# Convolution tail and conditioning units of a four-layer encoder trunk: second matrix fetched inside the channel blocks, partial sums multiplied as one chain

## The chip, the core and the metric

One core of a Trainium2 chip runs the whole program in one launch. The metric is the device time of that launch in microseconds (us), as the median of several runs. TensorE is written PE in the profile (PEld is its weight load), VectorE DVE, ScalarE ACT, GpSimd POOL and SyncE SP; SP issues nearly all of the DMAs.

## What is computed

The reference runs four layers over 256 tokens of 1024 channels. The mixer of a layer is attention (layers 0 and 3), a Conformer convolution module (layer 1) or a causal pooling mixer (layer 2); after each mixer comes a feed-forward block (FF) of 4096 channels with a squared ReLU. Each sub-layer adds `gate * rmsnorm(y)` to x and starts from `rmsnorm(x) * (1 + scale) + shift`; shift, scale and gate of all layers come from one conditioning vector:

```
c_act = silu(c)
mod = c_act @ ada_w[i] + ada_b[i]            # (1024) @ (1024, 6144), each layer
sh_m, sc_m, gt_m, sh_f, sc_f, gt_f = split(mod, 6)
# convolution module
a = h @ w_pw1 + b_pw1
u = a[:, :D] * sigmoid(a[:, D:])
u = causal_depthwise_conv(u, w_dw, width 31) + b_dw
u = silu(layernorm(u, ln_g, ln_b))
y = u @ w_pw2 + b_pw2
```

## The kernel before

**Products.** Every weight tile (128 x 1024, float32) is fetched into one of five `raw` buffers (`fetch`, L155) and split by `load` into a high part (ACT, L173) and a low part (DVE, L174); six buffers hold high parts, six low parts. A product is three matmuls: high times high, low times high, high times low (`mm3`, L583, L586 and L587).

**Conditioning units.** The matrix `ada_w` is read in units of 128 rows by 2048 columns (1 MB each, four `araw` buffers, L197). Eight units make a group, a group makes one row of shift, scale or gate values. `ada(n, vec)` takes n units. A unit outside `vec` is multiplied on PE at once (`ada_mm`, L265): four matmuls j = 0 to 3, each with a 32-column weight tile, into four partition strips of one bank of PSUM. A unit inside `vec` is added on DVE to two running sums `acc` (first half of the columns, then second half, L221 and L223), and `ada_flush` multiplies these sums by ones with the same four matmuls; j // 2 picks the half. `ada_fetch(n)` issues the DMAs of n units; `ada` issues one itself when none is waiting. A flush comes at the end of a group, and wherever a stretch that keeps sums on DVE ends. The tables `MIX` and `FF` say how many units each part takes: a list (for FF, one number for each of its 16 chunks; for the convolution, one for each of its eight channel blocks and one for its tail), then the units in the boundary ahead of the part, then the units fetched ahead near its end. In every boundary the units are multiplied on PE. 88 units are consumed in all.

**Feed-forward.** Each chunk c makes 256 hidden channels: two columns of h (L652 and L655, `colhalf`), relu and square on ACT, the split into `gh` and `gl`, the units of that chunk behind it on DVE, then the product with w2 of the chunk before (L583 to L587, `y`). At chunk 14 (`CF`) the units of the next part are fetched ahead. Boundary: the squares of y, the update of x, the norm, and the transposes into the next input (`transposed0`, L395; `transposed1`, L412).

**Convolution.** Eight channel blocks m. In each: fetch of the first matrix's tile of block m + 2; the product (`colblock`, L600 to L606); sigmoid (L1095) and gate (L1097); the block is written to DRAM and read back shifted as `u4` (L1100, L1079) one block later; the depthwise taps of an earlier block (L1060) and their transposes into token order, `ctok` (L1065); the units; and the broadcast of the gate row once it exists (`gate_row`). The tail has the taps of the last two blocks for each half t of the tokens, the LayerNorm (statistics L1126 and L1128, root on POOL L115 and L121, `un` L1132), transposes (L1149), Silu (L1155), the split (L1158, L1159) and the second matrix in two `rowblock`s of four tiles. The bias `b_pw2` is split like a weight and put into `y` by two matmuls with one row of ones for each quarter of y (L1143, L1144).

**Order of the work.** SP issues in the order of the text. On the other engines a planner orders the instructions at build time by its own cost figures and by their place in the text; `nosync(a, b)` and `line(engine, a)` put a behind b on its engine without a semaphore. An engine runs its instructions in the order so made.

Of the kernel before, what the change touches and what calls it, by code (L numbers as in the profile page):

```python
# [16 lines left out]
ALU = mybir.AluOpType  # L17
# [6 lines left out]
NT = S // P  # L24
KT = D // P
# [26 lines left out]
def tile_trunk(ctx: ExitStack, tc: tile.TileContext, x, cT, pos, invf, ada_w, ada_bg,  # L52
# [100 lines left out]
    def fetch(src):  # L153
        raw = raws.tile([P, D], F32, tag="raw", name="raw")[0:src.shape[0], 0:src.shape[1]]
        nc.sync.dma_start(raw, src)  # L155
        fetched[(src.tensor.name, src.offset)] = raw
# [3 lines left out]
    def load(src, pre=None, lined=False):  # L160
        key = (src.tensor.name, src.offset)
        if key in loaded:
            return loaded.pop(key)
        o = (slice(0, src.shape[0]), slice(0, src.shape[1]))
        if key not in fetched:
            fetch(src)
        raw = fetched.pop(key)
        if pre is not None:
            pre(raw)
        h = his.tile([P, D], F32R, tag="hi", name="hi")[o]  # L170
        l = los.tile([P, D], F32R, tag="lo", name="lo")[o]
        put = (lambda ins, eng: line(eng, ins)) if lined else after
        put(A.copy(h, raw), "act")  # L173
        put(V.tensor_tensor(l, raw, h.bitcast(F32), op=ALU.subtract), "dve")  # L174
        gate["free"] -= 1
        return h, l


    rows = {}
# [80 lines left out]
    def ada_mm(lhsT, raw, stop):  # L260
        first = "pt" not in grp
        if first:
            grp["pt"] = bank("ada", "adap")
        for j in range(4):
            mm = T.matmul(grp["pt"][32 * j:32 * j + 32, :], lhsT, raw[j // 2][:, HALF[j % 2]],  # L265
                          start=first, stop=stop)
            if gate["pe"] is not None:
                nosync(mm, gate["pe"])
        gate["ada"] = mm
# [66 lines left out]
    def prep(row):  # L336
        bcast("a", row, 1)
        bct["sh"] = row
# [701 lines left out]
    def conv(i, h, units, ahead, first):  # L1040
        j = i // 3
        hh, hl = h
        with tc.tile_pool(name=f"conv{i}", bufs=1) as vp:
# [42 lines left out]
            for m in range(KT):  # L1086
                if m + 2 < KT:
                    for p in range(2):
                        fetch(w_pw1[j, m + 2, p])
                if m == 0:  # L1090
                    hb = turned(first, vp.tile([P, 512], F32, tag="uc", name="r0", bufs=2), A.copy)
                else:
                    hb = colblock(w_pw1[j, m], hh, hl, "pw1")
                sg = vp.tile([P, S], F32, tag="sg", name="sg", bufs=2)
                sgi = A.activation(sg, hb[:, S:], AF.Sigmoid, bias=vecs["b1"][:, 8 + m:9 + m])  # L1095
                u = up[m % 3]
                V.scalar_tensor_tensor(u[:, 30:286], hb[:, :S], vecs["b1"][:, m:m + 1], sg,  # L1097
                                       op0=ALU.add, op1=ALU.mult)
                ud = dr.tile([4, 32, 288], F32, tag="ud", name="ud")
                nc.sync.dma_start(ud.rearrange("b r t -> (b r) t"), u)  # L1100
                uds.append((m, ud))
                if m > 0:
                    pend.append(spread_taps(*uds.pop(0)))
                if m > 0:
                    dgs.append(diags(m - 1))
                if len(pend) == 2:
                    taps(*pend.pop(0), dgs.pop(0), 0, S)
                ada(units[m], vec=ALL)
                gate_row(i)
            pend.append(spread_taps(*uds.pop(0)))  # L1110
            dgs.append(diags(KT - 1))
            b2h, b2l = load(b_pw2[j])
            wp = [load(w_pw2[j, k]) for k in range(4)]
            nosync(A.activation(vp.tile([P, 1], F32, name="warm"), vecs["lb"][:, 0:1], AF.Silu),
                   sgi)
            for t in range(NT):
                for p, dg in zip(pend, dgs):
                    taps(*p, dg, t * P, P)
            prep(rows[(i, 2)])
            shift_rows()  # L1120
            sh_, sl_ = planes()
            un = []
            for t in range(NT):
                st = sm.tile([P, 2, 6], F32, tag="st", name="st")
                for n in range(2):
                    V.bn_stats(st[:, n], ctok[t][n])  # L1126
                mv = sm.tile([P, 2], F32, tag="mv", name="mv")
                V.bn_aggr(mv, st)  # L1128
                r = rsqrt_eps(mv[:, 1:2])
                xn = tmp.tile([P, D], F32, tag="xa", name="un")  # L1130
                for n in range(2):
                    V.tensor_scalar(xn[:, 512 * n:512 * n + 512], ctok[t][n], mv[:, 0:1], r,  # L1132
                                    ALU.subtract, ALU.mult)
                un.append(xn)
            ada(units[8])
            ada_flush()
# [1 line left out]
            y = y_banks()  # L1138
            for t in range(NT):
                ts = slice(t * P, (t + 1) * P)  # L1140
                for n in range(2):
                    ns = slice(512 * n, 512 * n + 512)
                    T.matmul(y[t][n], ones_r, b2h[:, ns], start=True, stop=False, skip_group_check=True)  # L1143
                    T.matmul(y[t][n], ones_r, b2l[:, ns], start=False, stop=False, skip_group_check=True)  # L1144
                for g in range(2):
                    b = bank("h", "sT_ps")
                    for k in range(4):
                        kk = 4 * g + k
                        T.transpose(b[:, k * P:(k + 1) * P], un[t][:, kk * P:(kk + 1) * P], ident)  # L1149
                    sv = vp.tile([P, 4, 264], F32, tag="u4", name="sv", bufs=3)  # L1150
                    sv = sv.rearrange("p a b -> p (a b)")[:, 0:512].rearrange("p (a b) -> p a b",
                                                                              a=4)
                    for k in range(4):
                        kk = 4 * g + k
                        A.activation(sv[:, k], b[:, k * P:(k + 1) * P], AF.Silu,  # L1155
                                     scale=vecs["lg"][:, kk:kk + 1], bias=vecs["lb"][:, kk:kk + 1])
                    o = (slice(None), slice(4 * g, 4 * g + 4), ts)
                    V.tensor_copy(sh_[o], sv)  # L1158
                    V.tensor_tensor(sl_[o], sv, sh_[o].bitcast(F32), op=ALU.subtract)  # L1159
            rowblock(wp, [sh_[:, k] for k in range(4)],  # L1160
                     [sl_[:, k] for k in range(4)], y, False, False, tiles_first=True)
            ada_fetch(ahead)
            rowblock([w_pw2[j, 4 + k] for k in range(4)], [sh_[:, 4 + k] for k in range(4)],
                     [sl_[:, 4 + k] for k in range(4)], y, False, True)
# [12 lines left out]
    def pool(i, head, consts, units, ahead):  # L1177
# [87 lines left out]

    MIX = {
        0: ([2, 4, 2, 3, 3, 2], 0, 1),
        1: ([0, 0, 2, 0, 1, 2, 1, 0, 1], 2, 3),
        2: (2, 4, 3),
        3: ([0, 0, 0, 0, 0, 0], 0, 0),  # L1270
    }
    FF = {
# [3 lines left out]
        3: ([0] * NFC, 0, 0),  # L1276
    }
    qgs = cp.tile([P, q_g.shape[0], 3], F32, name="qgs")
# [139 lines left out]
```

## Time and profile before

| | |
|---|---|
| runs, us | 1173.12, 1180.72, 1184.35; median 1180.72 |
| profiled execution, us | 1184.47, span 1182.6 |
| PE busy | 1138.4 us, 96% of the span |
| PEld busy | 923.5 us, 78% |
| DVE busy | 850.6 us, 72% |
| ACT busy | 645.3 us, 55% |
| POOL busy | 54.1 us, 5% |
| mean granted TensorE clock | 0.983 |
| DMA | 290.00 MB, mean 245 GB/s |

The busy share says which engine is nearly always in use; where in the span it is not, and where it works at a lower clock, is seen only by stretches. The ends of matmuls in the profile are modelled, so the distance from one start to the next is the better measure of PE's pace.

### The profile page before, as it was taken

What the parts mean: (1) busy time and instruction counts of PE and PEld (TensorE: products, weight loads), DVE (VectorE), ACT (ScalarE), POOL (GpSimd) and SP (SyncE); (2) the same over time, 40 slices, a digit from 0 to 9 for tenths busy, and PEclk for the clock granted to TensorE, in tenths of its full rate; (3) what the DMA queues carried; (4) which work ended last, traced back from release to release, by engine and by line L of the source; (5) the groups of instructions that cost most, each with busy time, mean ns of one, the idle gap of its engine ahead of it and who ended that gap; (6) DMA issues with size and microseconds to landing.
All of it is one profiled execution on the core that took longest, in us unless ns stands there. A gap on an engine that the chain in (4) does not pass through costs nothing. (4 is left out here: it accounts for less than half of the span.)

```text
span 1182.6 us, 17593 instructions
## 1 busy us (share of the span) xinstructions
PE 1138.4 (96%) x6706; PEld 923.5 (78%) x6706; DVE 850.6 (72%) x1197; ACT 645.3 (55%) x1145; POOL 54.1 (5%) x127
## 2 busy tenths in 40 slices
PE   7899999999999999999999999999997999999997
PEld 4667778788778867888887677878877878888886
DVE  3689787877766665787876778787876995755554
ACT  3355576556553244755564366555545675756553
POOL 1000010000010010000000110000011001000000
PEclk9999999999999988999999899999998999999999
DMA  9878759787617785778896479888644522766550
GB/s 332 304 290 311 298 208 347 270 329 290 245 53 236 256 322 213 272 272 351 315 343 256 187 278 364 311 311 323 246 134 157 170 81 80 250 199 191 183 193 35
DMA packets 73383, 290.00 MB, mean 245 GB/s; under 512 B 9986, under 2 KB 15234, under 8 KB 61012
## 3 DMA queue, kind: packets, MB, share of 16 engines
q1 hardware_dynamic: 70484, 280.44, 65.1%
q0 software_dynamic: 2816, 8.46, 2.0%
q8 instruction: 52, 0.85, 0.3%
q14 instruction: 31, 0.25, 0.1%
HBM read 286.57 MB, written 2.29 MB: 244 GB/s over the span
## 5 line engine op out<-in xcount | busy, mean ns | idle before, releaser
L174 DVE TENSOR_TENSOR lo<-raw,hi 128x1024 fp32r<-128x1024 f32 (+2 forms) x335 | 392.0, 1192 | 98.4 <-ACT hi L173 69.0
L173 ACT CAST hi<-raw 128x1024 fp32r<-128x1024 f32 (+2 forms) x335 | 335.1, 1028 | 78.6 <-PE y L587 39.4
L652 PE MATMUL h<-hT,hi 128*128 128x512 f32 x960 | 240.4, 392 | 0.0
L652 PEld LDWEIGHTS h<-hT,hi 128*128 128x128 f32 x960 | 175.8, 188 | 37.7 <-issue 3.4
L583 PE MATMUL y<-hi,gh 128*128 128x512 f32 x512 | 200.3, 393 | 1.5 <-ACT hi L173 1.5
L586 PE MATMUL y<-lo,gh 128*128 128x512 f32 x512 | 200.1, 391 | 0.2
L587 PE MATMUL y<-hi,gl 128*128 128x512 f32 x512 | 199.0, 390 | 0.0
L655 PEld LDWEIGHTS h<-hT,lo 128*128 128x128 f32 x960 | 131.0, 190 | 14.9 <-issue 5.9
L704 ACT COPY r<-h 128x256 f32<-128x256 f32 x120 | 44.5, 371 | 175.8 <-PE h L655 175.7
L655 PE MATMUL h<-hT,lo 128*128 128x256 f32 x960 | 136.0, 283 | 0.0
L223 DVE SCALAR_TENSOR_TENSOR acc<-araw,c_act,acc 128x1024 f32<-128x1024 f32 x106 | 130.7, 1279 | 0.4 <-DMA araw<-in_ada_w_dram 0.4
L583 PEld LDWEIGHTS y<-hi,gh 128*128 128x128 f32 x512 | 96.3, 188 | 22.8 <-ACT hi L173 2.4
L587 PEld LDWEIGHTS y<-hi,gl 128*128 128x128 f32 x512 | 96.1, 188 | 21.8 <-issue 0.8
L586 PEld LDWEIGHTS y<-lo,gh 128*128 128x128 f32 x512 | 96.4, 188 | 18.5 <-DVE lo L174 1.0
L705 DVE TENSOR_TENSOR r<-h,r 128x256 f32<-128x256 f32 x120 | 50.5, 421 | 39.8 <-ACT r L704 39.2
L710 DVE TENSOR_TENSOR gl<-r,gh 128x512 fp32r<-128x512 f32 x60 | 41.4, 690 | 50.2 <-ACT gh L709 50.2
L706 ACT ACTIVATE r<-r 128x512 f32<-128x512 f32 x60 | 37.9, 632 | 35.2 <-DVE r L705 35.2
L583 PE MATMUL y<-hi,hT 128*128 128x512 f32 x96 | 39.4, 412 | 0.0
L707 ACT ACTIVATE r<-r 128x512 f32<-128x512 f32 x60 | 37.9, 632 | 1.7
L586 PE MATMUL y<-lo,hT 128*128 128x512 f32 x96 | 38.8, 405 | 0.0
L587 PE MATMUL y<-hi,hT 128*128 128x512 f32 x96 | 38.6, 404 | 0.0
L709 ACT CAST gh<-r 128x512 fp32r<-128x512 f32 x60 | 37.2, 620 | 1.4
(257 smaller groups left out, 1486.8 us busy)
## 6 DMA issues: line engine op xcount, KB each, us to landing
raw<-in_w_dram SPq DMA_DIRECT2D x256, 512.0 KB, 5.8
araw<-in_ada_w_dram SPq DMA_DIRECT2D x96, 1024.0 KB, 6.4
raw<-in_w_pw_dram SPq DMA_DIRECT2D x24, 512.0 KB, 5.7
raw<-in_w_o_dram SPq DMA_DIRECT2D x16, 512.0 KB, 3.2
u<-ud SPq DMA_DIRECT2D x32, 132.0 KB, 2.8
raw<-in_w_ukv_dram SPq DMA_DIRECT2D x8, 512.0 KB
bc_g<-rowd POOLq DMA_DIRECT2D x8, 512.0 KB, 4.0
bc_a<-rowd POOLq DMA_DIRECT2D x7, 512.0 KB, 6.7
```

Of the source, the lines that this page charges most:

```text
L173: put(A.copy(h, raw), "act")
L174: put(V.tensor_tensor(l, raw, h.bitcast(F32), op=ALU.subtract), "dve")
L223: V.scalar_tensor_tensor(acc, raw[:, sl], ck, acc, op0=ALU.mult, op1=ALU.add)
L583: mm = T.matmul(o, ah, bh, start=start, stop=False, skip_group_check=True)
L586: T.matmul(o, ah, bl, start=False, stop=False, skip_group_check=True)
L587: return T.matmul(o, al, bh, start=False, stop=stop, skip_group_check=True)
L652: T.matmul(b, w(0, kk), pair[:, :, kk], start=(kk == 0), stop=False, skip_group_check=True)
L655: T.matmul(b[:, 0:S], w(1, kk), pair[:, 0, kk], start=False, stop=(kk == KT - 1), skip_group_check=True)
L704: A.copy(rf, hb[:, S:])
L705: V.tensor_tensor(rf, hb[:, 0:S], rf, op=ALU.add)
L706: A.activation(r, r, AF.Relu)
L710: gli = V.tensor_tensor(gl, g2, gh.bitcast(F32), op=ALU.subtract)
```

## The change

The four matmuls of a unit or of a flush are put in the order j = 2, 3, 0, 1, each held behind the one before it. In the convolution the first four tiles of the second matrix are fetched in channel blocks 6 and 7; the broadcast of the next scale row and the transposes of the next shift row move from the tail to block 2; the bias is fetched after them and used as it is, unsplit, in one float32 matmul for each quarter of y, placed after the first `rowblock`; the LayerNorm's DVE steps are held in the order of the text. The units are dealt out anew: the three boundaries ahead of layer 1's convolution, layer 1's FF and layer 2's FF take one unit instead of two, layer 0's FF takes 17 instead of 15, layer 1's FF 21 instead of 17, layer 2's FF 17 instead of 20; the convolution takes 7 as before, with one in each of blocks 6 and 7 and none in the tail. All 88 are still consumed.

```diff
@@ ada_mm @@
-        for j in range(4):
+        mm = None
+        for j in (2, 3, 0, 1):
+            prev = mm
             mm = T.matmul(grp["pt"][32 * j:32 * j + 32, :], lhsT, raw[j // 2][:, HALF[j % 2]],
                           start=first, stop=stop)
+            if prev is not None:
+                nosync(mm, prev)
@@ conv, in the loop over m @@
                 if m + 2 < KT:
                     for p in range(2):
                         fetch(w_pw1[j, m + 2, p])
+                else:
+                    for k in range(2):
+                        fetch(w_pw2[j, 2 * (m + 2 - KT) + k])
+                if m == 2:
+                    prep(rows[(i, 2)])
+                    shift_rows()
@@ conv, behind the loop @@
-            b2h, b2l = load(b_pw2[j])
             wp = [load(w_pw2[j, k]) for k in range(4)]
+            fetch(b_pw2[j])
+            bias = fetched.pop((b_pw2[j].tensor.name, b_pw2[j].offset))
...
-            prep(rows[(i, 2)])
-            shift_rows()
...
-                    V.bn_stats(st[:, n], ctok[t][n])
+                    line("dve", V.bn_stats(st[:, n], ctok[t][n]))
...
-                V.bn_aggr(mv, st)
+                line("dve", V.bn_aggr(mv, st))
...
-                    V.tensor_scalar(xn[:, 512 * n:512 * n + 512], ctok[t][n], mv[:, 0:1], r,
-                                    ALU.subtract, ALU.mult)
+                    line("dve", V.tensor_scalar(xn[:, 512 * n:512 * n + 512], ctok[t][n],
+                                                mv[:, 0:1], r, ALU.subtract, ALU.mult))
...
-                for n in range(2):
-                    ns = slice(512 * n, 512 * n + 512)
-                    T.matmul(y[t][n], ones_r, b2h[:, ns], start=True, stop=False, skip_group_check=True)
-                    T.matmul(y[t][n], ones_r, b2l[:, ns], start=False, stop=False, skip_group_check=True)
...
             rowblock(wp, [sh_[:, k] for k in range(4)],
-                     [sl_[:, k] for k in range(4)], y, False, False, tiles_first=True)
+                     [sl_[:, k] for k in range(4)], y, True, False, tiles_first=True)
+            for t in range(NT):
+                for n in range(2):
+                    T.matmul(y[t][n], ones_f[0:1], bias[:, 512 * n:512 * n + 512], start=False,
+                             stop=False, skip_group_check=True)
@@ tables @@
-        1: ([0, 0, 2, 0, 1, 2, 1, 0, 1], 2, 3),
+        1: ([0, 0, 2, 0, 1, 2, 1, 1, 0], 1, 3),
...
-        0: ([1, 1, 1, 1, 1, 2, 1, 1, 1, 1, 1, 1, 1, 1, 0, 0], 1, 3),
-        1: ([1, 1, 1, 2, 1, 1, 2, 1, 1, 2, 1, 1, 1, 1, 0, 0], 2, 4),
-        2: ([1, 1, 1, 1, 2, 1, 2, 1, 2, 1, 1, 2, 1, 2, 1, 0], 2, 0),
+        0: ([1, 1, 2, 1, 1, 2, 1, 1, 2, 1, 1, 1, 1, 1, 0, 0], 1, 3),
+        1: ([2, 1, 1, 2, 1, 2, 1, 2, 1, 2, 1, 2, 1, 2, 0, 0], 1, 4),
+        2: ([1, 1, 1, 1, 1, 1, 1, 1, 1, 1, 2, 1, 1, 2, 1, 0], 1, 0),
```

## Rows read from the trace of the kernel before

**Rows 1.** Busy time by stretch: stretch, length, each engine's busy time, clock, DMA.

```profile
core 0: us, PE busy (x) PEld busy (x) DVE busy (x) ACT busy (x) POOL busy (x), PEclk, DMA share, GB/s
500.00:600.00 100.00, 100.00 (x500) 82.18 (x499) 81.68 (x88) 57.11 (x79) 2.19 (x4) 1.00 0.82 311
700.00:800.00 100.00, 99.96 (x513) 82.13 (x512) 82.26 (x94) 60.05 (x87) 1.48 (x3) 1.00 0.85 318
```

**Rows 2.** The same view, of the convolution's third block and its tail.

```profile
360.00:370.00 10.00, 8.97 (x106) 8.06 (x109) 4.57 (x6) 4.25 (x6) 0.00 (x0) 1.00 0.93 301
432.00:436.00 4.00, 3.71 (x67) 3.05 (x58) 3.08 (x3) 2.10 (x7) 0.39 (x1) 1.00 1.00 410
436.00:450.00 14.00, 14.00 (x44) 8.54 (x42) 7.70 (x15) 7.18 (x19) 1.17 (x2) 0.53 0.90 358
450.00:455.00 5.00, 5.00 (x23) 4.09 (x22) 2.28 (x3) 1.69 (x2) 0.00 (x0) 0.96 0.52 163
```

**Rows 3.** The same view, for the matmuls of L265 alone (PE, PEld, clock, DMA).

```profile
219.00:224.00 5.00, 2.10 (x8) 0.29 (x8) 1.00 0.19 77
...
635.00:640.00 5.00, 1.07 (x8) 0.16 (x8) 1.00 1.01 410
...
865.00:870.00 5.00, 2.10 (x8) 0.29 (x8) 1.00 0.43 125
418.00:422.00 4.00, 2.10 (x8) 0.29 (x8) 1.00 0.90 226
```

**Rows 4.** Timeline of PE, one flush of layer 0's FF: start, length, what.

```profile
310.40 1.05 PE L265 MATMUL adap<-acc,ones_c 128*32 128x512 f32 x4 [0.69 <-DVE acc L223]
311.38 0.73 PE L652 MATMUL h<-hT,hi 128*128 128x512 f32 x2
312.05 1.05 PE L265 MATMUL adap<-acc,ones_c 128*32 128x512 f32 x4
```

**Rows 5.** Timeline of PE, a unit's first matmul in layer 0's attention.

```profile
69.22 1.04 PE L265 MATMUL adap<-araw,c_act 128*32 128x512 f32 x2
```

**Rows 6.** Waits of PE over the whole span: sum, times, longest.

```profile
PE hT_ps L412 <- DVE xa L406: 8.6, 11, 3.6
PE adap L265 <- DVE acc L223: 1.7, 2, 1.0
```

**Rows 7.** Groups of DVE instructions, whole span: busy us, mean ns, idle before.

```profile
L223 DVE SCALAR_TENSOR_TENSOR acc<-araw,c_act,acc 128x1024 f32<-128x1024 f32 x106 | 130.7, 1279 | 0.4 <-DMA araw<-in_ada_w_dram 0.4
```

**Rows 8.** End of layer 1's FF: a wait of SP, DVE's, SP's and PE's timeline.

```profile
SPq L197 <- DVE acc L223: 16.7, 2, 8.4
629.55 2.48 DVE L223 SCALAR_TENSOR_TENSOR acc<-araw,c_act,acc 128x1024 f32<-128x1024 f32 x2
632.48 12.87 SPq L155 DMA_DIRECT2D raw<-in_w_dram  x8
639.60 0.73 PE L583 MATMUL y<-hi,gh 128*128 128x512 f32 x2 [1.52 <-ACT hi L173]
```

**Rows 9.** Timeline of DVE in the convolution's tail.

```profile
432.43 0.81 DVE L1132 TENSOR_SCALAR un<-ctok,mv,r 128x512 f32<-128x512 f32 x1 [1.02 <-POOL r L121]
433.16 2.35 DVE L174 TENSOR_TENSOR lo<-raw,hi 128x1024 fp32r<-128x1024 f32 x2
...
436.42 0.81 DVE L1132 TENSOR_SCALAR un<-ctok,mv,r 128x512 f32<-128x512 f32 x1
```

**Rows 10.** Timeline of PE in the convolution's tail.

```profile
433.37 0.94 PE L345 MATMUL sh_ps<-ident,row 128*128 128x2 f32 x7
434.61 0.17 PE L345 MATMUL sh_ps<-ident,row 128*128 128x2 f32 x1 [0.29 <-issue]
...
436.16 1.44 PE L265 MATMUL adap<-araw,c_act 128*32 128x512 f32 x8
```

**Rows 11.** Groups of PE instructions, 433 to 446 us: the split bias.

```profile
L1143 PE MATMUL y<-hi,ones_r 1*128 1x512 f32 x4 | 2.9, 717 | 0.0
L1144 PE MATMUL y<-lo,ones_r 1*128 1x512 f32 x4 | 2.3, 564 | 0.0
```

**Rows 12.** Timeline of PE in layer 2: an unsplit bias, two of four quarters.

```profile
668.85 1.98 PE L1251 MATMUL y<-raw,ones_f 1*128 1x512 f32 x4
```

**Rows 13.** DMA issues: a timeline of SP; KB each and us to landing.

```profile
417.75 3.73 SPq L1079 DMA_DIRECT2D u<-ud  x8
...
u<-ud SPq DMA_DIRECT2D x32, 132.0 KB, 2.8
```

## The prediction

> **What bounds the kernel now.** I read the busy time by stretch first. In the FF stretches PE is busy all the time at the full clock while DVE has about 18% left [rows 1]: there only fewer or better packed PE instructions shorten the time. Next the same view of the convolution's tail [rows 2]. PE idles 0.29 us in the four before 436 us at a granted clock of 1.00, then works at 0.53 until 450 us, nearly all of it at the lower level of 1.2 GHz. The loss is 14 x 0.47 + 5 x 0.04 = 6.8 us. Third, the matmuls of L265 alone [rows 3]. There are eight flushes in FF parts. Seven keep PE busy for 2.10 us (the first and the last are shown), one, in the stretch 635 to 640 us, for 1.07 with as many instructions. The timeline says why [rows 4]: the two matmuls of the first column half run in 1.05 us, two of h come between, and the two of the second half take 1.05 again; PE even waited 0.69 for DVE's first sum. Two instructions alone take 1.04 [rows 5]. So a run of such matmuls costs about 1.05 whether it holds one, two or all four of them. Last, waits: in boundaries PE waits for DVE's `xa` (8.6 us over eleven waits) [rows 6], and at the end of layer 1's FF for a split weight [rows 8].
>
> **The change part by part**, against the profiled execution of 1184.47 us (span 1182.6), which lies 3.75 above the runs' median of 1180.72; the sum is carried over to that median as it is.
>
> *Chain of four.* It starts with the half that DVE finishes last, so all four come into one run. Seven flushes lose one run: 7 x 1.05 = 7.4 us less [rows 3, 4], on a PE that has no idle time. The first matmul now needs the second sum, 1.28 us after the first [rows 7], and the FF's matmuls stand behind it in PE's order. The planner puts it after that sum by its own figures, and of the seven only two met a wait, 1.7 us together [rows 6]; I take nothing for waits, with bounds from the 1.7 given back to 7 x 1.28 = 9.0 lost. In layer 0's attention the units come in mixed runs; I take 0, within 1 either way (one run).
>
> *Units moved.* Three boundaries lose a unit on PE (a run of 1.07 [rows 3]). PE waits for `xa` in the boundaries [rows 6], a chain over ACT, POOL and DVE that the unit is not part of, so a shorter fill is a longer wait: 0, bounds -3.2 and 0. The tail's unit on PE gives way to a flush, 1.44 against 1.07 [rows 3, 10]: -0.4. Four units more go to DVE, 4 x 2 x 1.279 = 10.2 us [rows 7], under PE's cover: layer 2's FF has taken 20 units, ones and twos in turn, and PE was busy 99.96 of 100 us [rows 1]. Without that cover a unit costs 2.6.
>
> *One flush more at the end of layer 0's FF*, as its last two units open a group: +1.1 [rows 3]. The third flush of layer 1's FF moves from chunk 15, where a 1.52 us wait follows it anyway, to chunk 13, ahead of the same wait: 0.
>
> *SP's queue at the end of layer 1's FF.* At chunk 14 SP issues four units ahead, into four buffers, before the last weights. SP waited 16.7 us in two waits for DVE to use units [rows 8]; the last was released by the unit of chunk 13 (done at 632.03), the weights went out at 632.48, and PE waited 1.52 us for the first of them. Chunk 13 now has two units, so the fourth buffer comes free 2 x 1.24 us later, and with it the weights, their splits and PE: +2.5, bounds 0 (DVE is early) and +2.5.
>
> *Shift row.* Eight matmuls and some waits, 433.37 to 434.70 [rows 10], leave the tail; in block 2 PE had 1.03 us idle [rows 2] that takes most of them: -1.0, bounds -1.3 and 0. Two broadcast DMAs go with them out of POOL's queue, where the tail's roots then have fewer ahead: 0.
>
> *Bias.* Eight short instructions, 2.9 + 2.3 us with overlaps and mostly at the lower clock [rows 11], give way to eight float32 ones, 1.98 for four [rows 12], so 4.0 at full clock: -0.2, bounds -1 and +1.5. Its split, 1.2 each on ACT and DVE, goes, hidden before. The tile stays in one of five raw buffers until used; SP's next FF weight stands behind it, with the first `rowblock` and more to land: 0, at worst the 1.52 of rows 8.
>
> *Splits earlier, norm in order.* The low parts leave the gap between the halves of `un` (432.43 and 436.42, 2.35 us of splits between [rows 9]), which brings the second half forward by some 3 us. PE was not idle there; what the earlier data change is the thin stretch of two-column, one-row and 32-column matmuls before the clock fell. I take half of the 6.8 as given back, -3.4, bounds -6.8 and 0.
>
> *Queue in blocks 6 and 7.* The four early fetches go out ahead of `ud` and `u4`; by then raw buffers are free as in blocks 0 to 5: 0. Block 7's unit is new, and its 1 MB goes out in front of the last four `u4`, which follow the first four at once today [rows 13] and land in 2.8 us. At 410 GB/s [rows 2] 1 MB takes 2.6 us. No row has this order; the bounds are 0 and +2.6, and I take +1.2, as the first taps of that block come a tap group later. The Trainium skill (DMA: Bandwidth & Descriptors, Queues, rings and completion order) says that the DMAs one engine issues share its rings and that a ring's descriptors are consumed in order. By it the full 2.6 would be paid and the time be 1174.5; no row here shows it.
>
> **The sum:** -7.4 - 0.4 + 1.1 + 2.5 - 1.0 - 3.4 - 0.2 + 1.2 = -7.6: 1176.9 for an execution like the profiled one, **1173.1** at the median.
>
> **The rivals.**
>
> *A clean tail.* The clock holds, `u4` is not late and the two waits for `acc` go: -7.6 - 3.4 - 1.2 - 1.7 = -13.9, or 1166.8; with weights in time at the end of layer 1's FF, 1164.3. For it: the shift row and the unit leave the thin stretch. Against: the bias puts 4 us of one-row matmuls into the tail, and the clock fell at 0.29 us of idle time in four [rows 2]. The Trainium skill (TensorE: Matmul & The Clock Gate, HAM oscillation) lays the lower clock to idle gaps between matmuls; by it this rival would hold. The rows speak against that reading here, so it stays behind the forecast.
>
> *The runs do not join,* or the chain only moves them: the 7.4 are gone and the new flush has two runs: -7.6 + 7.4 + 1.05 = +0.9, 1181.6. This is also the case in which the change does not do what it says. For it: the four were put apart by a planner whose figures no view shows.
>
> *The chain is pulled apart (slower).* If the planner frees each matmul only behind the one before, others may come between all four: four runs of 1.05 for each flush in an FF. Then seven flushes cost 2.1 more instead of 1.05 less and the two new or moved ones 3.1 more each: -7.6 + 7.4 + 14.7 + 6.2 = +20.7, 1201.4. With three runs it is half of that, about 1192, so it decides from three runs on. For it: in layer 0's attention one matmul did stand alone [rows 5], and the flush of the convolution took 2.10 [rows 3]. Against: seven of eight FF flushes had two runs, with DVE's two sums as the reason.
>
> **How the numbers follow.** Forecast 0.42, clean tail 0.26, runs not joined 0.17, pulled apart 0.15. A run of this kernel differs by about 1% from another, so 1% (11.8 us) is about what a measurement can tell from no change. The forecast's own range is 1167 to 1179; with the clean tail's better end and the unjoined runs and some spread of the runs the range is 1162 to 1187, leaving out the last case and a little at the lower end. Faster by over 1% is below 1168.9: the clean tail and 0.06 of the forecast, 0.32. Slower by over 1% is the last case, 0.15. The rest is 0.53.
>
> **What would show it.** L265 at 1.07 us in each FF flush, one run of eight instructions, with at most small waits for `acc`: the chain is right; 2.1 or 4 says which rival. A granted clock of 1.00 throughout the tail: clean; a fall after the bias: the forecast or worse. The wait for a split weight before `y` at the end of layer 1's FF: 4.0 instead of 1.52. A wait of L1060 for `u` in the last taps: the queue. PE waiting for `lo` in layer 1's FF, or DVE full there for several chunks, would make the prediction wrong, since 21 units there are taken as hidden.

## The result and the profile after

| | before | after |
|---|---|---|
| median of the runs, us | 1179.51 (1173.12 to 1184.35, four runs) | **1194.28** (1193.41 to 1195.33, four runs) |
| ratio after / before, 95% interval | | 1.0123 [1.0087, 1.0159] |
| profiled execution: span, us | 1182.6 | 1191.6 |
| PE busy, us | 1138.4 | 1130.0 |
| span less PE busy, us | 44.2 | 61.6 |
| mean granted clock | 0.983 | 0.976 |

The change makes the kernel slower, by 14.8 us in the medians and 9.0 us in the two profiled executions; the forecast was 1173.1 us, and the measured time lies above its range. The rows of PE's busy and idle time are the shortest account: PE has 8.4 us less work (most of it the chain) and 17.4 us more idle time. The profiled execution of before (1184.47 us) is slower than each of its four runs, and that of after (1193.41) is the fastest of its four, so what follows by stages explains the 9.0 us between these two and not the 14.8.

The same stretches as in [rows 1, 2], as near as the new times allow, and two more (PE, PEld, DVE, ACT and POOL busy, then clock, DMA share, GB/s):

```profile
500.00:600.00 100.00, 100.00 (x514) 83.59 (x513) 85.32 (x95) 58.64 (x82) 2.23 (x4) 1.00 0.93 349
...
423.00:437.00 14.00, 9.25 (x145) 7.38 (x146) 3.82 (x4) 0.37 (x1) 0.00 (x0) 0.64 1.02 353
437.00:450.00 13.00, 10.09 (x155) 7.88 (x148) 8.87 (x17) 7.47 (x20) 1.58 (x4) 0.89 0.43 175
...
640.00:650.00 10.00, 2.90 (x21) 1.74 (x20) 4.35 (x8) 3.40 (x6) 0.00 (x0) 0.77 0.98 392
...
700.00:712.00 12.00, 8.03 (x40) 7.37 (x41) 7.03 (x13) 5.63 (x15) 2.52 (x6) 0.57 0.17 68
```

The middle of layer 1's FF is as full as before. The holes are elsewhere: 4.75 of 14 us idle in the convolution's tail at a clock of 0.64, with the DMA engines full; 7.1 of 10 us at the end of layer 1's FF; 4 of 12 us behind the pooling stage. In each the clock is low as well; the clock has two levels in these traces, 1.00 (2.4 GHz) and 0.50 (1.2 GHz), and a value between them is a mean.

The flushes, as in [rows 3] (PE, PEld, clock, DMA, for the matmuls of L267 alone, which is L265 of before):

```profile
219.00:224.00 5.00, 1.07 (x8) 0.16 (x8) 1.00 0.85 319
...
431.00:436.00 5.00, 1.94 (x8) 0.23 (x8) 0.50 1.00 423
...
877.00:882.00 5.00, 1.06 (x8) 0.16 (x8) 1.00 0.45 135
```

Every flush in an FF is one run of eight instructions, 1.06 to 1.07 us. The one of 1.94 is the convolution's last, at half the clock. What PE waits for, over the whole span (sum, times, longest; [rows 6] has `xa` and `acc` of before, [rows 8] the 1.52 us for `hi`; the last line is the wait for `dg` of before):

```profile
PE hT_ps L399 <- ACT dg L393: 7.1, 2, 6.3
PE y L587 <- ACT hi L173: 7.1, 1, 7.1
...
PE adap L267 <- DVE acc L223: 4.2, 2, 3.9
...
PE sT_ps L1154 <- DVE un L1141: 2.5, 1, 2.5
```

```profile
PE hT_ps L395 <- ACT dg L389: 1.4, 2, 1.2
```

By stages on PE, after less before: up to the convolution's input (the first transposes of L412, L416 of after) -2.2; to the end of the first matrix's products +3.1, where a flush and the shift row's matmuls now stand that were in the tail (e3, with the tables alone, has +3.5 there); from there to the end of the last tap 24.9 against 17.2, **+7.7**; the rest of the tail and the boundary -2.4; from the input of layer 1's FF to the pooling stage's first matmul 194.8 against 188.7, **+6.1**; from there to the next FF's input +1.9; layer 2's FF -3.6; layer 3's attention -1.5; the rest -0.1. The sum is +9.0. The ends of the two tail stretches, before and then after:

```profile
414.17 2.08 PE L606 MATMUL pw<-hT,hi 128*128 128x256 f32 x16
431.68 1.76 PE L1060 MATMUL dw_ps<-u,dg 128*32 128x128 f32 x54
```

```profile
415.08 2.07 PE L610 MATMUL pw<-hT,hi 128*128 128x256 f32 x16
440.31 1.75 PE L1064 MATMUL dw_ps<-u,dg 128*32 128x128 f32 x54
```

**End of layer 1's FF.** SP's timeline and one of its waits (compare [rows 8]):

```profile
623.81 17.81 SPq L197 DMA_DIRECT2D araw<-in_ada_w_dram  x4
641.71 12.08 SPq L155 DMA_DIRECT2D raw<-in_w_dram  x8
```

```profile
SPq L197 <- DVE acc L223: 19.9, 3, 12.1
```

SP stands 17.81 us at the four units fetched ahead, and the weights go out when they have gone. In the last 7.7 us of that time the DMA engines have little to do (the share of 0.21; columns as above) and PE is still full:

```profile
634.00:641.70 7.70, 7.70 (x46) 6.57 (x48) 7.35 (x8) 1.51 (x3) 0.00 (x0) 1.00 0.21 66
```

DVE's timeline says what SP waits for:

```profile
634.65 1.23 DVE L174 TENSOR_TENSOR lo<-raw,hi 128x1024 fp32r<-128x1024 f32 x1 [0.25 <-ACT hi L173]
635.80 0.68 DVE L714 TENSOR_TENSOR gl<-r,gh 128x512 fp32r<-128x512 f32 x1
636.40 4.87 DVE L223 SCALAR_TENSOR_TENSOR acc<-araw,c_act,acc 128x1024 f32<-128x1024 f32 x4
```

The two units of chunk 13 are used from 636.40 to 641.27, and the weights leave at 641.71. PE then waits 7.10 us for the first split weight, and the clock falls during that wait, at 645.4, for 10.2 us.

**Convolution's tail.** SP, then PE, then DVE (compare [rows 13], where eight `u4` go out in one piece of 3.73 us):

```profile
418.63 2.09 SPq L1083 DMA_DIRECT2D u<-ud  x4
420.77 0.43 SPq L197 DMA_DIRECT2D araw<-in_ada_w_dram  x1
421.31 2.35 SPq L1083 DMA_DIRECT2D u<-ud  x4
```

```profile
423.32 3.51 PE L1064 MATMUL dw_ps<-u,dg 128*32 128x128 f32 x64 [1.46 <-DMA u<-ud]
...
431.60 1.94 PE L267 MATMUL adap<-acc,ones_c 128*32 128x512 f32 x8 [3.91 <-DVE acc L223]
```

```profile
428.97 2.48 DVE L223 SCALAR_TENSOR_TENSOR acc<-araw,c_act,acc 128x1024 f32<-128x1024 f32 x2 [4.63 <-DMA araw<-in_ada_w_dram]
```

Block 7's unit goes out at 420.77, and DVE gets it at 428.97. It ends a group, so its flush waits 3.91 us, and the remaining taps stand behind the flush in PE's order until 433.27.

### The profile page after: what moved, and what is told of

Same layout as the page of the kernel before. It is cut to its first block, busy times and chain, and to the rows that moved or that the text cites. A ratio compares the mean times of both kernels' runs of the same rounds, so it can differ in the third digit from the quotient of the medians.

```text
span 1191.6 us, 17585 instructions
## 1 busy us (share of the span) xinstructions
PE 1130.0 (95%) x6690; PEld 924.1 (78%) x6690; DVE 856.2 (72%) x1204; ACT 643.7 (54%) x1144; POOL 53.3 (4%) x127
## 5 line engine op out<-in xcount | busy, mean ns | idle before, releaser
L174 DVE TENSOR_TENSOR lo<-raw,hi 128x1024 fp32r<-128x1024 f32 (+1 forms) x334 | 391.6, 1192 | 101.6 <-ACT hi L173 71.9
L173 ACT CAST hi<-raw 128x1024 fp32r<-128x1024 f32 (+1 forms) x334 | 334.9, 1029 | 86.2 <-PE y L591 43.1
L223 DVE SCALAR_TENSOR_TENSOR acc<-araw,c_act,acc 128x1024 f32<-128x1024 f32 x110 | 135.7, 1278 | 4.7 <-DMA araw<-in_ada_w_dram 4.6
L518 DVE TENSOR_TENSOR v<-y,bc_g 128x512 f32<-128x512 f32 x32 | 21.9, 688 | 31.4 <-ACT junk L135 27.0
```

Source lines behind the costliest of these rows:

```text
L223: V.scalar_tensor_tensor(acc, raw[:, sl], ck, acc, op0=ALU.mult, op1=ALU.add)
```

## The experiments

Idle is the span less PE's busy time, from the profiled execution of each kernel, and so is the clock; the median and ratio come from all its runs. The kernel before was run beside each; its medians there lie between 1178.93 and 1179.88 us, and the ratio is to that median.

| kernel | median, us | ratio to before | idle, us | clock |
|---|---|---|---|---|
| after | 1194.28 | 1.0123 [1.0087, 1.0159] | 61.6 | 0.976 |
| e1 chain alone | 1172.43 | 0.9929 [0.9901, 0.9957] | 44.7 | 0.988 |
| e2 convolution's edits alone | 1186.71 | 1.0052 [1.0030, 1.0074] | 50.4 | 0.984 |
| e3 new tables alone | 1201.63 | 1.0173 [1.0130, 1.0216] | 62.5 | 0.980 |
| e4 chain and convolution's edits | 1177.92 | 0.9972 [0.9948, 0.9997] | 53.3 | 0.986 |
| e5 after, FF's end eased | 1191.95 | 1.0107 [1.0069, 1.0144] | 58.0 | 0.978 |
| e6 after, no unit in block 7 | 1186.24 | 1.0059 [1.0032, 1.0086] | 58.6 | 0.977 |
| e7 as e4, late fetches | 1174.45 | 0.9948 [0.9928, 0.9968] | 47.8 | 0.983 |
| e8 as e1, chunk 13 empty | **1167.78** | 0.9907 [0.9878, 0.9936] | 42.1 | 0.985 |
| e9 after, three places mended | 1188.52 | 1.0084 [1.0052, 1.0116] | 57.6 | 0.977 |
| e10 as e8, shift row and norm | 1170.58 | 0.9930 [0.9907, 0.9953] | 45.3 | 0.985 |
| e11 as e10, bias unsplit | 1173.76 | 0.9952 [0.9929, 0.9975] | 45.1 | 0.987 |
| e12 as e9, 17 units in layer 1's FF | 1183.40 | 1.0036 [1.0008, 1.0064] | 48.4 | 0.977 |

### The change in its parts: e1 to e4

e1 is the kernel before with the chain alone:

```diff
-        for j in range(4):
+        for j in (2, 3, 0, 1):
...
+                nosync(mm, prev)
```

> The kernel before with nothing but the chain j = 2, 3, 0, 1. Theory A (the chain joins the flushes; the loss of the whole change lies in the tables and the tail): seven FF flushes go from 2.10 to 1.07 us of PE and the time falls by 6 to 9 us, ratio 0.992 to 0.995. Theory B (the chain makes PE stand behind DVE's second sum): the time rises by 1 to 9 us, with waits of PE for acc above the 1.7 us of before.

Measured: -7.45 us (1172.43 against 1179.88; the interval is -5.1 to -11.7); seven runs of 1.05 are 7.4. A flush of layer 2's FF in its profile, and the waits for the sums over the whole span (0.9 the longest):

```profile
849.00:856.00 7.00, 1.06 (x8) 0.16 (x8) 1.00 0.48 141
```

```profile
PE adap L267 <- DVE acc L223: 1.5, 2, 0.9
```

The waits did not grow from the 1.7 us of [rows 6]; DVE's second sum is not late. In the profiled execution the clock did not fall in the tail; one profile can't say how often that is so.

e2 is the kernel before with all edits of the convolution, without chain and new tables:

```diff
+                else:
+                    for k in range(2):
+                        fetch(w_pw2[j, 2 * (m + 2 - KT) + k])
+                if m == 2:
+                    prep(rows[(i, 2)])
+                    shift_rows()
...
-                    T.matmul(y[t][n], ones_r, b2h[:, ns], start=True, stop=False, skip_group_check=True)
+                    T.matmul(y[t][n], ones_f[0:1], bias[:, 512 * n:512 * n + 512], start=False,
```

> The kernel before with the convolution's edits alone (early fetches, shift row in block 2, unsplit bias, LayerNorm in order), loop over j and tables as before. Theory A (the tail lost its time to the unit in block 7 that the tables put there): the tail is not longer than before, from the end of the first matrix's products to the last taps 17 us or less, and the time lies within 0 to 5 us below before. Theory C (the edits of the tail are what costs): the last taps come 5 to 9 us later than before and the time rises by 4 to 9 us.

Measured: +6.8 us, as theory C has it; from the last product to the last tap it took 22.6 us against 17.2. In the tail PE waited 4.1 us for `u` in two waits, where before it had waited 1.0. The edits that were to give 4.6 us cost something instead.

e3 is the kernel before with the new tables alone:

```diff
-        1: ([0, 0, 2, 0, 1, 2, 1, 0, 1], 2, 3),
+        1: ([0, 0, 2, 0, 1, 2, 1, 1, 0], 1, 3),
...
-        1: ([1, 1, 1, 2, 1, 1, 2, 1, 1, 2, 1, 1, 1, 1, 0, 0], 2, 4),
+        1: ([2, 1, 1, 2, 1, 2, 1, 2, 1, 2, 1, 2, 1, 2, 0, 0], 1, 4),
...
```

> The kernel before with the new tables alone. Theory A: slower by 10 to 16 us, of which 5 to 6 are a longer wait of PE for a split weight at the end of layer 1's FF (7 us against 1.5) and 3 to 6 the convolution's tail, where a flush waits for the unit of block 7. Theory C: within 3 us of before.

Measured: +21.75 us, the largest effect of any part and more than I had expected. Three waits of PE make most of it visible: 6.3 us for `u` in the tail, 5.7 for a split weight at the end of layer 1's FF, 6.0 for `dg` behind the pooling stage. The flush in the tail waits only 0.8 here; without the chain block 7's unit shows in the wait for `u`.

e4 is the changed kernel with the old tables:

```diff
-        1: ([0, 0, 2, 0, 1, 2, 1, 1, 0], 1, 3),
+        1: ([0, 0, 2, 0, 1, 2, 1, 0, 1], 2, 3),
...
```

> The changed kernel with the tables of before. Theory A: the loss is gone, 1167 to 1175 us, faster than before by 5 to 12. Theory C (tail edits cost) or B (chain costs): 1180 or more.

Measured: 1177.92 us. So the tables cost 16.4 us on top of the other edits, but the convolution's edits cost 5.5 on top of the chain (the two intervals just touch), and the theory that the tables hold all of it falls. Its own profile shows why, in SP's timeline and its waits from 405 to 428 us:

```profile
405.19 0.43 SPq L197 DMA_DIRECT2D araw<-in_ada_w_dram  x1
407.32 2.71 SPq L155 DMA_DIRECT2D raw<-in_w_pw_dram  x2
412.19 0.33 SPq L1110 DMA_DIRECT2D ud<-up  x1
412.61 9.76 SPq L1083 DMA_DIRECT2D u<-ud  x8
```

```profile
SPq L1083 <- DMA ud<-up: 6.1, 1, 6.1
```

A unit and two early weight tiles, 2 MB together, go out ahead of a 144 KB write of `ud`. The reads of `u4` need that write; SP waits 6.1 us for it, and PE 5.0 us for `u`. In the changed kernel itself this wait does not occur: there the write goes out at 418.21, almost 6 us after the last early tile, and between 405 and 428 us SP waits 9.4 us for `up` and 1.3 for a weight buffer, and not for `ud`.

### The early fetches: e7

e7 is e4 without the fetches in blocks 6 and 7; the four tiles are fetched in the tail as before.

```diff
-                else:
-                    for k in range(2):
-                        fetch(w_pw2[j, 2 * (m + 2 - KT) + k])
```

> Chain and the convolution's edits with the tables of before, but the first four tiles of the second matrix fetched behind the last shifted reads, as before. Theory G (the early fetches stand ahead of the shifted reads in SP's queue): the waits of the taps for u fall from 5.0 us to about 1, and the time falls from 1178 by 2 to 6, to 1172 to 1176. Rival (the late reads have another reason, the bias or the order of the norm cost): within 1.5 us of 1178.

Measured: 1174.45 us, -3.5 against e4, with overlapping intervals; from the last product to the last tap it takes 19.0 us against 23.9. SP no longer waits for the write (landed in 2.6 us), and issues the eight reads at once; PE's wait for `u` is 0.7:

```profile
416.79 0.34 SPq L1107 DMA_DIRECT2D ud<-up  x1
417.23 3.71 SPq L1083 DMA_DIRECT2D u<-ud  x8
```

### Block 7's unit: e6

e6 is the changed kernel with block 7's unit taken in block 3.

```diff
-        1: ([0, 0, 2, 0, 1, 2, 1, 1, 0], 1, 3),
+        1: ([0, 0, 2, 1, 1, 2, 1, 0, 0], 1, 3),
```

> The changed kernel, with the unit of the convolution's block 7 taken in block 3. Theory F (block 7's 1 MB comes late and goes out ahead of the last shifted reads): PE's wait for acc in the tail (3.9 us) goes, the waits for u fall by 1 us or more, and the time falls by 3 to 7, to 1187 to 1191 us. Theory C (the tail's own edits cost): the tail is as long as before this edit, within 2 us.

Measured: 1186.24 us, 8.0 below the changed kernel. The wait of the flush for `acc` is gone from the convolution. The wait for `u` did not fall, as I had expected, but rose from 1.5 to 3.0, and that for `un` stays. The early fetches are not shown as the cause of the 3.0: SP has no wait for `ud` here, and e9, without them, still waits 2.3 for `u`.

```profile
PE dw_ps L1064 <- DMA u<-ud: 3.0, 1, 3.0
PE sT_ps L1154 <- DVE un L1141: 2.5, 1, 2.5
```

### The end of layer 1's FF: e5 and e8

e5 is the changed kernel with chunk 13's second unit taken in chunk 10.

```diff
-        1: ([2, 1, 1, 2, 1, 2, 1, 2, 1, 2, 1, 2, 1, 2, 0, 0], 1, 4),
+        1: ([2, 1, 1, 2, 1, 2, 1, 2, 1, 2, 2, 2, 1, 1, 0, 0], 1, 4),
```

> The changed kernel, with one of the two units of chunk 13 of layer 1's FF taken at chunk 10, so that 12 and 13 have one each as before. Theory D (SP's queue: the four units fetched ahead wait for buffers of the last chunks' units, and the last weights stand behind them): PE's wait for a split weight at the end of that FF falls from 7.1 to 1.5 to 3 us, the low clock from 645 us goes, and the time falls by 4 to 9, to 1185 to 1190 us. Theory E (DVE is full with 21 units, and the weights are late for want of splits): the wait stays at 5 or more and the time within 2 us of the changed kernel's 1194.

Measured: 1191.95 us, 2.3 below the changed kernel, and the intervals overlap. The mechanism holds in part: SP's stand at the four units went from 17.81 to 12.57 us, but PE still waited twice:

```profile
PE y L587 <- ACT hi L173: 4.6, 2, 3.8
```

e8 asks the same of the better kernel: e1 with nothing to use in chunk 13, its unit taken in chunk 11.

```diff
-        1: ([1, 1, 1, 2, 1, 1, 2, 1, 1, 2, 1, 1, 1, 1, 0, 0], 2, 4),
+        1: ([1, 1, 1, 2, 1, 1, 2, 1, 1, 2, 1, 2, 1, 0, 0, 0], 2, 4),
```

> The kernel before with the chain alone, and the unit of chunk 13 of layer 1's FF taken at chunk 11, so that chunk 13 has none. Theory D: the fourth buffer comes free a chunk earlier, the wait of 1.5 us for a split weight at that FF's end goes, and the time falls by 1 to 4 us from the chain's 1172. Theory E: no change of that wait.

Measured: 1167.78 us, 4.7 below e1, the lowest median of all, but the intervals of the two overlap. What the profile shows is the mechanism: SP's last stand at the units goes from 9.17 to 7.24 us, the weights leave at 611.13 instead of 617.74, and PE's wait for `hi` of 1.5 us does not occur there any more:

```profile
603.79 7.24 SPq L197 DMA_DIRECT2D araw<-in_ada_w_dram  x2
611.13 17.20 SPq L155 DMA_DIRECT2D raw<-in_w_dram  x8
```

### Is that all? e9 and e12

e9 mends the three places together in the changed kernel: no early fetches, block 7's unit in block 3, chunk 13 empty at 21 units.

```diff
...
-        1: ([0, 0, 2, 0, 1, 2, 1, 1, 0], 1, 3),
+        1: ([0, 0, 2, 1, 1, 2, 1, 0, 0], 1, 3),
...
-        1: ([2, 1, 1, 2, 1, 2, 1, 2, 1, 2, 1, 2, 1, 2, 0, 0], 1, 4),
+        1: ([2, 1, 1, 2, 1, 2, 1, 2, 2, 2, 2, 2, 1, 0, 0, 0], 1, 4),
```

> The changed kernel with its three suspected places mended together: the four early fetches of the second matrix left out, block 7's unit taken in block 3, and in layer 1's FF the unit of chunk 13 taken earlier so that chunk 13 takes none (21 units in all, as after). Theory H (these three places hold all that the new tables and the early fetches cost): about -8 for the unit, -3.5 for the fetches, -4 to -6 for the FF's end against 1194.3, so 1175 to 1179 us, near the kernel with chain and tail edits on the old tables without the early fetches (1174.5). Rival I (a shift of units to other places costs by itself, through DVE or the boundaries): still above 1184 with all three waits gone.

Measured: 1188.52 us, a clear miss of my theory, and not below e6, which mends only one of the three (1186.24; the intervals overlap). Three waits for split weights stand where one stood, and the stretch from 600 to 640 us is no longer full:

```profile
PE y L587 <- ACT hi L173: 6.0, 3, 3.2
```

```profile
600.00:640.00 40.00, 35.31 (x165) 28.20 (x164) 28.22 (x32) 19.02 (x30) 0.00 (x0) 0.91 0.76 281
```

With five chunks in a row of two units each, SP waits for a free buffer chunk by chunk (8.5 us in two waits for `acc` between 585 and 606), and the weights stand behind. The number 21 alone does not do that: the changed kernel has it too, with ones and twos in turn, and there PE is busy 41.62 of 41.70 us from 600 to 641.7.

e12 is e9 with those four units put into layer 2's FF.

```diff
-        1: ([2, 1, 1, 2, 1, 2, 1, 2, 2, 2, 2, 2, 1, 0, 0, 0], 1, 4),
+        1: ([1, 1, 1, 2, 1, 1, 2, 1, 1, 2, 1, 2, 1, 0, 0, 0], 1, 4),
-        2: ([1, 1, 1, 1, 1, 1, 1, 1, 1, 1, 2, 1, 1, 2, 1, 0], 1, 0),
+        2: ([1, 1, 1, 1, 2, 1, 2, 1, 2, 1, 2, 2, 1, 2, 1, 0], 1, 0),
```

> As the changed kernel with its three places mended (1188.5 us), and the four units that layer 1's FF takes more than before put back into layer 2's FF: layer 1's FF takes 17 units with none in chunk 13, layer 2's FF 21. Theory M (in layer 1's FF 21 units are too many: a unit whose buffer is not yet free holds SP, the weights stand behind it, and PE waited 6.0 us in three waits for split weights there): those waits go, and with them the falls of the clock at 605 and 622 us, so about -7 to -9, 1180 to 1182 us. If the gate row's broadcast in the pooling stage (6.5 us of waiting) also goes back to its old order, 1175 to 1179. Rival N (the count does not matter; the boundaries with one unit and layer 0's FF with 17 are what costs): 1186 to 1190.

Measured: 1183.40 us, -5.1 with intervals that overlap a little; the waits for `hi` are gone, and the wait for `dg` behind the pooling stage fell from 6.5 to 2.1 us. A part of the price is the number of units in that FF or the way they follow each other, less than I expected; e12 changes both. It still lies 9.0 us above e7, which differs from it by the rest of the tables (boundaries with one unit, a unit in block 3, 17 and 21 units in layer 0's and layer 2's FF). No run separates these.

The clocks of the single runs say more about these 9.0 us than the two profiles do. e12's ten runs have a mean granted clock between 0.969 and 0.979, e7's ten between 0.981 and 0.989; the means of the ten are 0.975 and 0.984. If PE works all through the stretches at the lower level, this difference is worth about 11 us of the span (an estimate from these clocks), which is as much as the whole gap. The kernels fall into the same two groups throughout: all with the new tables or parts of them (after, e3, e5, e6, e9, e12) have means of 0.975 to 0.979 over their runs, all with the old tables, with e8's one moved unit or without, 0.983 to 0.986. Which of the moved units lowers the clock, and where in the span, stays open.

### The tail's other edits: e10 and e11

e10 is e8 with the shift row in block 2 and the norm's DVE steps in order, bias split, fetches late.

```diff
+                if m == 2:
+                    prep(rows[(i, 2)])
+                    shift_rows()
...
-                    V.bn_stats(st[:, n], ctok[t][n])
+                    line("dve", V.bn_stats(st[:, n], ctok[t][n]))
...
```

> The best version so far (chain, chunk 13 of layer 1's FF without a unit; 1167.8 us) with two of the tail's edits: the shift row in block 2 and the LayerNorm's DVE steps in order. The bias stays split and the second matrix is fetched as before. Theory J (these two take only idle steps out of the tail): -1 to -3, 1165 to 1167 us. Rival K (the earlier normalised half only brings PE into the taps' and the splits' way, and any edit of the tail is within 1 us of nothing): 1167 to 1169. If it is over 1170, the shift row's matmuls in block 2 or the fixed order of DVE cost.

Measured: 1170.58 us. The gain of 1 to 3 us that I expected did not come; against e8 it is 2.8 us more, with overlapping intervals, so a loss isn't shown either. The profiles say the same of the tail: from the first matrix's last product to the FF's input it takes 56.0 us here and 56.3 in e8.

e11 is e10 with the unsplit bias.

```diff
-                    T.matmul(y[t][n], ones_r, b2h[:, ns], start=True, stop=False, skip_group_check=True)
-                    T.matmul(y[t][n], ones_r, b2l[:, ns], start=False, stop=False, skip_group_check=True)
...
+                    T.matmul(y[t][n], ones_f[0:1], bias[:, 512 * n:512 * n + 512], start=False,
+                             stop=False, skip_group_check=True)
...
```

> As the run before it, and the bias unsplit behind the first rowblock. Theory J2 (bias -0.2, as predicted; bounds -1 and +1.5): within 1.5 us of that run. Rival L (the unsplit bias is what makes the tail edits cost about 2 us beside the chain alone): 2 to 3 us above that run, about 1169 to 1171.

Measured: 1173.76 us, 3.2 above e10, as rival L has it, again with overlapping intervals. In the profiles the stretch from the last product to the FF's input takes 61.4 us, 5.4 more than in e10. The windows of e11 around the bias say more than the times (same columns as above; the bias is PE's only work from 448.36 to 453.40):

```profile
445.00:448.36 3.36, 3.36 (x16) 2.50 (x14) 2.46 (x3) 2.47 (x3) 0.00 (x0) 1.00 0.72 267
448.36:450.50 2.14, 2.14 (x6) 1.03 (x6) 1.23 (x1) 0.08 (x1) 0.00 (x0) 1.00 0.13 54
450.50:453.40 2.90, 2.90 (x5) 0.68 (x3) 0.00 (x0) 0.00 (x0) 0.00 (x0) 0.50 0.00 0
453.40:457.30 3.90, 3.90 (x10) 3.13 (x10) 0.00 (x0) 0.00 (x0) 0.00 (x0) 0.50 0.71 250
```

```profile
448.36 5.09 PE L1166 MATMUL y<-raw,ones_f 1*128 1x512 f32 x8
453.39 0.80 PE L587 MATMUL y<-hi,hT 128*128 128x512 f32 x1
```

Two us into a closed run of one-row matmuls the clock falls to 0.50, with PE recorded as busy throughout, and stays there for 6.8 us. In the profiles of all nine kernels with the unsplit bias a fall begins within the bias run or at most 1.3 us behind it (in after at 464.5, the run ending at 463.3; in e7 at 454.3, ending at 453.8). In e1, e8 and e10, with the split bias strewn between transposes and products, the clock does not fall in the tail. The split is no safeguard, though: in the kernel before and in e3 it fell as well, at 436.7 and 445.2 us, with the split bias in progress.

## Why the prediction was wrong, step by step

**Chain of four: right,** in mechanism and size (-7.4 forecast, -7.45 measured, e1; -8.8 in e4 against e2). That the numbers agree to 0.1 us is chance, with an interval of -5.1 to -11.7. Both rivals about it, that the runs do not join and that the chain is pulled apart, are false: every flush in an FF is one run of eight.

**"SP's queue at the end of layer 1's FF": right in mechanism, size wrong.** The term was +2.5, which was also its upper bound; the stage became 6.1 us longer. Counted from the start of this FF's input (477.4 before, 483.6 after), the weights left at 155.1 and now at 158.1: 3.0 later, near the 2.5. PE ran out of work at 160.7 before and at 159.1 now, since joined flushes stand ahead of the wait. From the weights' issue to the first product it took 7.12 us and now 8.05. So 3.0 + 1.6 + 0.9 = 5.5 of the 5.58 by which the wait grew. The sum had counted the chain's gain and the queue's loss side by side; ahead of a wait that ends late, a gain on PE only lengthens the wait. What it had no term for is the clock: it fell during the longer wait and stayed low until 655.6, so that PE worked 5.8 us at half speed, a loss of 2.9 us (an estimate from the granted clock).

**"Units moved ... under PE's cover": wrong.** The cover was read off PE's and DVE's busy shares [rows 1], and DVE has indeed room. And in the changed kernel the cover holds in the middle of layer 1's FF. The limit that was overlooked is SP's single order of issue: where a unit's buffer is not yet free, SP waits and the weights stand behind it, at the end of that FF here (7.1 us of PE's time) and in its middle when five chunks in a row have two units (e9: 6.0 us in three waits; e12, with 17 units and no such sequence, has none). That layer 2's FF takes 20 was no proof for layer 1's, since it has no units to fetch ahead at its end.

**"Queue in blocks 6 and 7": the largest error in the tail.** Early fetches were taken as 0; with the old tables they cost about 3.5 us (e4 against e7, overlapping intervals), since 2 MB in front hold up the small write and reads that the taps need. In the changed kernel SP had no such wait, so what they cost there is open. Block 7's unit was taken as +1.2, at most 2.6; it costs 8.0 (after against e6). This is the step that failed: I looked at what stood behind its transfer and not at its own user: the unit ends a group, its flush stands ahead of the last taps, and it came to DVE only 8.2 us after its issue. The Trainium skill (DMA: Bandwidth & Descriptors, Queues, rings and completion order) says that DMAs of one engine share its rings and that these are consumed in order. e4 and e7 agree with it: the wait for `ud` is 6.1 us with 2 MB ahead and absent without the early fetches. The order is not all of it: e9, which leaves them out too, still has a wait of 2.3 us for `ud`.

**"Splits earlier, norm in order" with the clock: not borne out.** I took -3.4. The edit did what it was to do on DVE: the two halves of the first `un` now follow each other at once, where 4.0 us lay between their starts before [rows 9]:

```profile
439.83 1.53 DVE L1141 TENSOR_SCALAR un<-ctok,mv,r 128x512 f32<-128x512 f32 x2 [1.01 <-POOL r L121]
```

But the last tap ended 8.6 us later than before, the clock fell four times from 423.5 to 464.5, after waits and after the bias, and nothing of the 6.8 us came back. Taking half of them rested on no row that tied the clock to the halves of `un`. **"Shift row"** (-1.0) is not borne out either: e10 has both edits, at a clock of 1.00 throughout the tail, and its tail is as long as e8's.

**"Bias": wrong side.** -0.2, bounds -1 and +1.5, from the instructions' durations; e11 against e10 gives +3.2 (overlapping intervals), with the fall of the clock in the run itself. I had written that 4 us of one-row matmuls speak against a clean tail, and yet did not price it.

**"Boundaries 0" and the rest.** Behind the pooling stage a gate row's broadcast arrives late: PE waited 6.31 us for `dg` after it, and that took the gain of a pooling stage in which the clock did not fall (before, it fell at 672.2 us for 10.2). Timeline of POOL, after:

```profile
685.98 1.18 POOL L321 DMA_DIRECT2D rowd<-row  x2
691.31 0.57 POOL L324 DMA_DIRECT2D bc_g<-rowd  x1 [4.15 <-DVE hT L1238]
```

The profile puts POOL's wait down to DVE, but in the kernel the broadcast follows the row's write `rowd` directly and needs it to have landed, and that is what became slow. The same two transfers of before and of after (KB each, us from issue to landing):

```profile
bc_g<-rowd POOLq DMA_DIRECT2D x1, 512.0 KB, 4.2
rowd<-row POOLq DMA_DIRECT2D x2, 4.0 KB, 1.7
```

```profile
bc_g<-rowd POOLq DMA_DIRECT2D x1, 512.0 KB, 7.5
rowd<-row POOLq DMA_DIRECT2D x2, 4.0 KB, 5.0
```

The DMA engines moved 408 GB/s around them (684 to 700 us) against 267 before (675 to 690); that this traffic is the reason is likely, but no run tests it. The prediction named this place nowhere. About 9 us of the tables' price (e12 against e7) go with a lower clock whose cause stays open.

**The rivals.** A clean tail stands in three profiles: in e1 and e8, where no edit of the tail was made, and in e10, where two of them were and the time is no lower than e8's. So the edits did not bring it, and all of them together, in the changed kernel, went with four falls. My slower rival gave 1201.4 us, not far from the result, for a reason that is false, so its nearness is luck; what the runs show is a queue, which I had only as bounds of single terms, not as a rival of its own, and a lower clock.

## What to carry to other kernels

Where one queue issues both the bulk that is fetched ahead and the small or urgent transfers, follow the order of issue: a transfer whose buffer is not yet free holds everything behind it, even while the DMA engines have little to do (a share of 0.21 at the end of layer 1's FF). Before an engine's spare time is filled, ask when each new piece arrives and who stands behind its consumer, not only whether the engine has room; the busy shares can't show it. A closed run of one-row matmuls is worth strewing between other work: in nine profiles of nine the clock fell in or just behind such a run. That strewing alone keeps the clock up isn't shown; it fell in two of the five kernels with the split bias too.

## What was not expected of the hardware

- The granted clock fell to 0.50 while PE was recorded as busy for 2.14 of 2.14 us, 2.1 us into a run of one-row float32 matmuls with full matmuls before it (e11). The Trainium skill (TensorE: Matmul & The Clock Gate, HAM oscillation) lays the lower clock to idle gaps between matmuls; this stretch shows a fall without a recorded one, and the measurement decides.
- A 144 KB write that landed in 2.6 us (e7) made SP wait 6.1 us for it when the same weights had been issued ahead of it on the same queue, with a unit, 2 MB in all (e4). In the changed kernel, where the write went out later, there was no such wait.
